# Router products in two halves of the array, row sums added up on VectorE, weight splits moved from GpSimd to VectorE, and one pool of eight PSUM banks

## The chip, the cores and the metric

The kernel runs on one core of one Trainium2 chip. The metric is the device time of one execution in microseconds (us). Below, PE is TensorE (its weight loads PEld), ACT is ScalarE, DVE is VectorE, POOL is GpSimd, and SP is the engine that issues most DMAs. The granted clock is the share of TensorE's full 2.4 GHz.

## The reference, cut to what matters

Two transformer blocks run in a row on 512 tokens of width 1024, in float32. The first block modulates and normalizes, mixes a dilated attention with a convolution, and ends in a mixture of 32 experts: a router picks one of 4 groups and two experts in it for each token, from a normalized row.

```
h2 = rms_norm(x, g_norm2) * (1 + sc2) + sh2
g_logits = h2 @ w_rg + b_rg          # 4 columns
e_logits = h2 @ w_re + b_re          # 32 columns
x = x + gt2 * hier_moe(h2, ...)
```

The second block puts 16 meta tokens in front (528 rows), runs a stick-breaking attention and a gated linear attention on projections of the same normalized rows, gates and mixes them, and adds the mix with a norm of its own; a convolutional feed-forward ends it.

```
mix = (gate_sb * (sb @ w_sb_out) + gate_gla * (o @ w_gla_out)) @ w_o
h = h + rmsnorm(mix, norm_mix_post)
```

Each rms norm needs the sum of squares over 1024 columns for every token.

## The kernel before, in words

Activations lie transposed: 8 tiles (m or k = 0 to 7) of 128 columns of the model by the tokens. Most products are made of three: a weight is split into a rounded high half on ACT (line 223) and the rest, its low half, on another engine (line 224, `ws.lo`), and so are the activations; high by high, high by low and low by high are added in PSUM (`mm3`, lines 310 to 312; line 1598 and 1620 for the projections). A plain float32 product goes to PE as two passes. Weights arrive through `Stream`: rings of 1 MB buffers that SP's DMAs fill as soon as a buffer comes free.

The order of instructions on each engine is settled when the program is built: a scheduler takes what is ready first by its estimates, in the order of the program where several are; a few places pin the order (`keep_in_program_order`) or raise a priority.

Four places matter.

The router (`router`, line 803) closes the first block's mixing. For each m, `ev_x1` makes xs (x scaled) and sq (x squared); `router` multiplies xs by 36 columns of router weights (line 808) and sq by ones, 32 columns wide, at partitions 64 to 95 of another bank (line 809), and both add up over m. `token_major` transposes xs on PE. At the end both sums are copied to `lgT`, and the selection of experts, a chain on DVE, begins; then come the experts, whose weights are some 196 MB from memory. Line 1206 multiplies there by two halves of 64 columns, line 1276 makes row sums with products of 32 columns.

After the experts the second block starts. Four splits of its value weights run through `ws` with the low half on POOL (line 1458 sets it; line 1731 sets it back to DVE); at the same time the scatter of the experts' rows (lines 1306, 1307, 1299), row sums (1276) and value products (`pva`, `pvb`) share PE, and `spread` (lines 1523 to 1529) distributes the row norms.

Then PSUM is laid out anew. Line 1733 opens a pool with four single banks (`p1`) and two pairs (`p2`). The first query and key projections (`pq`, line 1598, two banks each) are made in it by `need(("s", 0))`. Lines 2003 and 2004 close it and open one of eight single banks, and `weave` (line 2005) interleaves the stick-breaking chain (`sb_gen`: pz products, ACT and DVE work, psb products), the other projections (`qkg`, three steps to each step of the chain) and the gated attention.

Last, the mixing stage (`mix_mm`, `mix_out`, lines 2170 to 2199): for 8 m and two halves a of the tokens, 24 products give `pmix`; ACT copies it and squares it, and `su.flush` sums the squares of all m over the partitions through products of 128x128 ones (line 1643). The norm that comes of it (`su.rstd`) feeds the feed-forward.

Of the kernel before, what the change touches and what calls it, by code (L numbers as in the profile page):

```python
# [11 lines left out]
F32 = mybir.dt.float32  # L12
# [3 lines left out]
OP = mybir.AluOpType  # L16
# [4 lines left out]
P = 128  # L21
T = 512
D = 1024
KD = D // P
NM = 16
L = T + NM
# [5 lines left out]


COLS = [
    ("b_mod", 48), ("g_norm1", 8), ("conv_b", 4), ("conv_ln_g", 4), ("conv_ln_b", 4),
    ("conv_w", 4 * 31), ("g_norm2", 8), ("w_router", 8 * 36), ("c", 8),
    ("g_final", 8), ("norm_mix_pre", 8), ("b_gk", 4), ("gla_head_norm", 2),
    ("norm_mix_post", 8), ("norm_ffn_pre", 8), ("conv_w2", 22 * 3), ("conv_b2", 22),
]
# [132 lines left out]
def weave(*gens):  # L172

    live = [[t, dt, g] for g, t, dt in gens]
    while live:
        x = min(live, key=lambda q: q[0])
        x[0] += x[1]
        if next(x[2], x) is x:
            live.remove(x)
# [14 lines left out]
def build(nc, tc, I, out, dbg=None):  # L194
    with ExitStack() as ctx:
        _build(ctx, nc, tc, I, out, dbg or {})


def _build(ctx, nc, tc, I, out, dbg):
    mm = nc.tensor.matmul  # L200
    transpose = nc.tensor.transpose
    act = nc.scalar.activation
    tt = nc.vector.tensor_tensor
# [105 lines left out]
    def mm3(ps, lh, ll, rh, rl, first, last):  # L309
        mm(ps, lh, rh, start=first, stop=False)  # L310
        mm(ps, lh, rl, start=False, stop=False)  # L311
        mm(ps, ll, rh, start=False, stop=last)  # L312
# [10 lines left out]
    def cc(name, i=0, n=1):  # L323
        o = COFF[name][0] + i
        return cpk1[:, o:o + n] if o < NCOL1 else cpk2[:, o - NCOL1:o - NCOL1 + n]
# [5 lines left out]
    ones = const.tile([P, P], F32, name="ones")  # L331
# [44 lines left out]
    def p1(name="p1"):  # L376
        return pp.tile([P, 512], F32, name=name, tag="p1", bufs=4)
# [105 lines left out]
    ws = Stream(plan, castp, 3, nmoe)  # L483
# [62 lines left out]
    for k in range(KD):  # L546
        sq = big.tile([P, T], F32, name="sq", tag=("sq", "t512")[k % 2], bufs=2)
# [211 lines left out]
    wr = lambda k: cc("w_router", 36 * k, 36)  # L759
# [24 lines left out]
    plg = []  # L784
# [18 lines left out]
    def router(st):  # L803
        m, sq, xs = st
        if m == 0:
            plg.extend((p1("plg"), p1("plq")))
            act(rs_[:, 0, 0:1], sq[:, 0:1], AF.Sqrt)
        mm(plg[0][0:36, :], wr(m), xs, start=(m == 0), stop=(m == KD - 1), skip_group_check=True)
        mm(plg[1][64:96, :], ones[:, 0:32], sq, start=(m == 0), stop=(m == KD - 1), skip_group_check=True)
        if m < KD - 1:  # L810
            token_major(m, xs)

    def token_major(m, xs):
        pt = p1("pth")
        for i in range(4):
            s = slice(i * P, (i + 1) * P)
            transpose(pt[:, s], xs[:, s], ident)
        for a in range(2):
            (copy if m % 2 and m < KD - 1 else lambda o, x: act(o, x, AF.Copy))(
                h2t[a][:, :2 * D].rearrange("p (i d) -> p i d", d=D)[:, :, m * P:(m + 1) * P],  # L820
                pt[:, a * 256:(a + 1) * 256].rearrange("p (i n) -> p i n", n=P))
# [77 lines left out]
    for m in range(KD):  # L899
# [12 lines left out]
        behind = ev_x1(m, ps)  # L912
    next(mod)
    router(behind)
    for m in range(KD):
        dump(f"x1_{m}", xT[m])
# [4 lines left out]
    plg = p1("plgt")[:, :256].rearrange("p (i n) -> p i n", n=64)  # L921
# [320 lines left out]
    def weighted(psd, w, spare=False):  # L1242
        yh, yl = [(ep.tile([P, D], F32R, name="yx", tag="x", bufs=3) if spare else
                   yp.tile([P, D], F32R, name=n, tag=n)) for n in ("yh", "yl")]
        for n in range(2):
            s = slice(n * 512, (n + 1) * 512)
            act(yh[:, s], psd[n], AF.Copy, scale=w)  # L1247
            stt(yl[:, s], psd[n], w, yh[:, s].bitcast(F32), OP.mult, OP.subtract)  # L1248
        return yh, yl
# [64 lines left out]
    side, xs = [], {}  # L1314
# [99 lines left out]
    last = weighted(psd, wsl[:, q:q + 1])  # L1414
# [4 lines left out]
    with tc.For_i(0, n_over, 1) as o:  # L1419
# [5 lines left out]
        ws = Stream([(I["w_moe"][bass.ds(e, 1), i, :, :].rearrange("a p n -> (a p) n"), (2048,), False)  # L1425
                     for i in range(6)])
# [13 lines left out]
    ws = main  # L1440
# [14 lines left out]
                self.t = raw1.tile([P, 2048], dt, name="wsplit", tag="raw", bufs=2)  # L1455
            return self.t[:, :1024] if tag == "whi" else self.t[:, 1024:]

    ws.pool, ws.rc, ws.rings, ws.lo = Halves(), 2, ws.rings[:1], nc.gpsimd.tensor_tensor
    ws.rings[0][3], ws.pin = len(plan), nmoe + 1
    ws.hold_at(nmoe + 2)  # L1460
    ws.load()
# [103 lines left out]
    HP = ctx.enter_context(tc.tile_pool(name="H", bufs=1))  # L1565
# [7 lines left out]
    def t5(name, p=P):  # L1573
        return HP.tile([p, L], F32, name=name, tag="t5", bufs=4)
# [8 lines left out]
    def psum_pool(name, n1, n2):  # L1583
        st = ExitStack()
        pool = st.enter_context(tc.tile_pool(name=name, bufs=1, space=PSUM))
        q1 = lambda name="p1": pool.tile([P, 512], F32, name=name, tag="p1", bufs=n1)
        q2 = lambda name="p2": pool.tile([P, 2, 512], F32, name=name, tag="p2", bufs=n2)
        return st, q1, q2
# [38 lines left out]
    def part(ap, a):  # L1627
        return ap[:, E[a][0]:E[a][1]]

    class Sums:  # L1630
# [7 lines left out]
        def add(self, a, sq):  # L1638
            self.pend[a].append(sq)

        def flush(self, a):
            for sq in self.pend[a]:
                mm(self.ps[a], ones, part(sq, a), start=(self.n[a] == 0), stop=(self.n[a] == KD - 1))  # L1643
                self.n[a] += 1
            self.pend[a] = []

# [55 lines left out]
    def vproj():  # L1702

        pst = []

        def gen():
            pst.extend(p1("pv") for _ in range(5))
            yield from vproj_gen(nh, nl, xt, pst[:4], pst[4])

        return gen(), lambda dst: vproj_end(dst, pst[:4], pst[4], t5("tail")[:, :T], p1)  # L1710
# [8 lines left out]
    for k0 in (0, 4):  # L1719
        for x in (nh, nl):  # L1720
            for a in range(2):
                for k in range(4):
                    mm(pl[a][32 * k:32 * k + 32], w[:, k0 + k, :], x[k0 + k][:, a * HF:(a + 1) * HF].bitcast(F32),
                       start=(k0 == 0 and x is nh), stop=(k0 > 0 and x is nl), skip_group_check=True)
# [5 lines left out]
        act(glr[:, a * HF:(a + 1) * HF], pl[a], AF.Copy)  # L1730
    ws.lo = tt
    PB.close()
    PS, p1, p2 = psum_pool("psumC", 4, 2)
    wgk = cp.tile([P, 512], F32, name="wgk")
    nc.gpsimd.memset(wgk, 0.0)
    for g in range(0, P, 32):
# [192 lines left out]
    def sb_gen():  # L1929
        units = [(hp, j, b) for hp in range(4) for j in (4, 3, 2, 1, 0) for b in range(2)]  # L1930
        yield from pipeline(units, [sb_z, sb_soft, sb_cum, sb_sum, sb_exp, sb_out])
# [64 lines left out]
    def gla_gen():  # L1996
        units = [(g, li) for g in range(2) for li in range(7)]
        yield from pipeline(units, [gla_diff, gla_exp, gla_mul, lambda un, gf: att_mm(un[1], un[0], gf, gf)])
# [1 line left out]
    need(("s", 0))  # L2000
    gv0, gv0_end = vproj()
    gv1, gv1_end = vproj()
    PS.close()
    PS, p1, p2 = psum_pool("psumC2", 8, 0)
    weave((sb_gen(), 0, 1), (qkg, 0, 0.33), (gla_gen(), 6.6, 1.6), (sb_meta(), 32.5, 1.6),
          (gv0, 41, 0.1))
    dump("sbT", sbT)
# [7 lines left out]
    last = gv0_end(gv[:, 0])  # L2015
# [3 lines left out]
    last = gv1_end(gv[:, 1])  # L2019
# [71 lines left out]
    PS, p1, p2 = psum_pool("psumE", 0, 4)  # L2091
# [18 lines left out]
    for d in range(2):  # L2110
        sqs = []
# [5 lines left out]
        for a in range(2):  # L2117
            for h in range(4):
                mm(pn[32 * h:32 * h + 32, a, :H5], ones[:, 0:32], ends(sqs[h])[:, a], start=(d == 0), stop=(d == 1),
                   skip_group_check=True)  # L2120
# [43 lines left out]
    PS, p1, p2 = psum_pool("psumF", 4, 2)  # L2164
    t = p2("psum")
    su = Sums([t[:, 0], t[:, 1]])
    r = HP.tile([P, L], F32, name="rstd2", tag="rstd2", bufs=2)
    wo, pso, sqo = {}, {}, {}

    def mix_mm(m, a):  # L2170
        if m not in wo:
            wo[m] = ws.nxt(P)
            sqo[m] = t5("sq")
        wh, wl = wo[m]
        ps = pso[m, a] = p1("pmix")[:, :E[a][1] - E[a][0]]
        for kk in range(KD):
            mm3(ps, wh[:, kk, :], wl[:, kk, :], part(mh[kk], a), part(ml[kk], a), kk == 0, kk == KD - 1)

    def mix_out(m, a):
        ps = pso.pop((m, a))  # L2180
        act(part(mx[m], a), ps, AF.Copy, scale=cc("norm_mix_post", m))
        act(part(sqo[m], a), ps, AF.Square)
        su.add(a, sqo[m])

    for m in range(KD - 2):
        for a in range(2):
            mix_mm(m, a)
            su.flush(a)
        for a in range(2):
            mix_out(m, a)  # L2190

    for a in range(2):
        for m in (KD - 2, KD - 1):
            mix_mm(m, a)
            su.flush(a)
            mix_out(m, a)
        su.flush(a)
        with tc.high_priority(offset=100):
            su.rstd(a, r, D)
# [8 lines left out]
    def h_gen(a):  # L2208
        for k in range(KD):
            with tc.high_priority(offset=200):  # L2210
                t, h, g = cp.tile([P, T], F32, name="t", tag="y", bufs=3)[:, :E[a][1] - E[a][0]], part(hT[k], a), cc("norm_ffn_pre", k)
                tt(t, part(mx[k], a), part(r, a), OP.mult)
                (nc.gpsimd.tensor_tensor if k in HPL else tt)(h, h, t, OP.add)
                act(part(nh[k], a), h, AF.Copy, scale=g)
                stt(part(nl[k], a), h, g, part(nh[k], a).bitcast(F32), OP.mult, OP.subtract)
            sq = t5("sq")
            act(part(sq, a), h, AF.Square)
            su.flush(a)
            su.add(a, sq)
            if k == KD - 1:  # L2220
                su.flush(a)
            yield
# [130 lines left out]
    su = Sums([p1("psum"), p1("psum")])  # L2353
# [29 lines left out]
```

## Time and profile before

| | |
|---|---|
| three runs | 1812.36, 1812.47, 1816.58 us; median 1812.47 |
| the profiled execution | 1818.69 us, span 1816.9 |
| PE busy | 1745.1 us, 96% of the span |
| DVE, ACT, POOL busy | 881.3, 629.3, 109.6 us |
| mean granted clock of PE | 0.978 |
| memory traffic | 322 MB read, 180 GB/s over the span |

The span is the time from the first to the last instruction of the profiled execution. A busy PE counts matmuls that overlap in its pipeline, so a matmul's duration is longer than its step: products of 512 columns that stand one behind the other have durations of about 0.4 us and starts 0.23 us apart. In a row of a timeline, the bracket at the end gives the idle time of the engine before the instruction and what ended it; several equal instructions are merged (x2). In a table of stretches the columns are the busy time of each engine with its number of instructions, the granted clock, the share of the DMA engines and GB/s. In a list of waits the numbers are the total, the count and the longest.

### The profile page before, as it was taken

To read this page: it belongs to the slowest core of one execution; us is meant where nothing else is said; L and a number is where in the kernel's file an instruction comes from. 1 tells how busy PE (TensorE), PEld (TensorE's weight loads), DVE (VectorE), ACT (ScalarE), POOL (GpSimd) and SP (SyncE) were. 2 spreads that over 40 slices of the span, in tenths; PEclk is the share of its full clock that TensorE was granted. 3 is DMA by queue.
4 is the path that set the end of the run, shared out by engine and by line. 5 is a ranking of instruction groups with operands and counts; after the bars stand their busy time and mean duration, and the time that the engine had idled before them with its cause. 6 is when DMAs were issued, how large, how long until landed. Compare 5 with 4: busy or idle time off the path is not lost.

```text
span 1816.9 us, 26870 instructions
## 1 busy us (share of the span) xinstructions
PE 1745.1 (96%) x10826; PEld 1263.2 (70%) x10826; DVE 881.3 (49%) x1597; ACT 629.3 (35%) x1141; POOL 109.6 (6%) x147
## 2 busy tenths in 40 slices
PE   7999997999999999998899999999999999999997
PEld 4776565444445444445788668989999899789985
DVE  6789654433333334235577742253332645335534
ACT  5226653211111111104567743242233633223322
POOL 2000010000000000003200100030000111001101
PEclk9989898999999999999999999999999999999998
DMA  8563253999999999930411012113222222222221
GB/s 327 199 242 136 89 216 130 380 409 409 408 411 360 385 408 410 412 128 27 159 67 49 24 47 93 47 63 128 102 100 87 70 91 78 100 93 93 94 87 64
DMA packets 73986, 328.01 MB, mean 181 GB/s; under 512 B 8019, under 2 KB 8403, under 8 KB 59652
## 3 DMA queue, kind: packets, MB, share of 16 engines
q1 hardware_dynamic: 72608, 320.36, 46.6%
q0 software_dynamic: 1248, 5.91, 0.9%
q8 instruction: 86, 1.41, 0.3%
q14 instruction: 40, 0.33, 0.0%
q10 hardware_dynamic: 4, 0.00, 0.0%
HBM read 321.98 MB, written 4.26 MB: 180 GB/s over the span
## 4 chain that ended last, share of the span: by engine, by line
PE 48%; DVE 3%; ACT 2%; DMA 1%; POOL 1%; issue 1%; DVEq 0%; ACTq 0%; POOLq 0%
PE p L1620 11%; PE pup L2232 7%; PE pq L1598 4%; PE pg L312 2%; PE pg L310 2%; PE pg L311 2%; PE pd L311 2%; PE pd L312 2%; PE pd L310 2%; PE pv L310 1%; PE pv L311 1%; PE pv L312 1%; PE pmix L310 1%; PE psum L1643 1%; PE pmix L312 1%; PE pmix L311 1%
## 5 line engine op out<-in xcount | busy, mean ns | idle before, releaser
L224 DVE TENSOR_TENSOR wsplit<-raw,wsplit 128x1024 fp32r<-128x1024 f32 (+1 forms) x140 | 167.4, 1198 | 250.6 <-ACT wsplit L223 244.7
L223 ACT ACTIVATE wsplit<-raw 128x1024 fp32r<-128x1024 f32 (+1 forms) x144 | 146.8, 1022 | 260.5 <-PE pd L312 76.3
L1206 PE MATMUL pgu<-raw,x 128*64 128x512 f32 x960 | 220.3, 598 | 0.0
L1206 PEld LDWEIGHTS pgu<-raw,x 128*64 128x64 f32 x960 | 64.1, 136 | 119.9 <-issue 106.4
L1299 DVE SCALAR_TENSOR_TENSOR x<-psx,modc,x 128x512 f32<-128x512 f32 x136 | 93.2, 745 | 50.1 <-PE psx L1307 50.0
L1248 DVE SCALAR_TENSOR_TENSOR yl<-pdn,wsl,yh 128x512 fp32r<-128x512 f32 x34 | 25.4, 751 | 178.8 <-ACT yh L1247 178.3
L1206 PE MATMUL pdn<-raw,hT 128*64 128x512 f32 x480 | 105.7, 593 | 0.7 <-ACT hT L1228 0.7
L1228 ACT ACTIVATE hT<-pht 128x512 f32<-128x512 f32 x17 | 10.2, 597 | 232.0 <-PE pht L1222 227.5
L1206 PEld LDWEIGHTS pdn<-raw,hT 128*64 128x64 f32 x480 | 34.5, 137 | 69.1 <-issue 64.4
L647 DVE SCALAR_TENSOR_TENSOR y<-u,cpk,y 128x512 f32<-128x512 f32 x116 | 80.6, 748 | 0.1
L311 PE MATMUL pd<-wsplit,ah 128*128 128x512 f32 x176 | 71.1, 404 | 2.1 <-DVE wsplit L224 2.0
L1168 PE MATMUL psg<-oh,h2h 128*128 128x256 f32 (+1 forms) x288 | 67.8, 292 | 3.1 <-DVE oh L1153 3.1
L1620 PE MATMUL p<-nha,wsplit 128*128 128x258 f32 x384 | 69.0, 293 | 1.3 <-ACT wsplit L223 0.7
L312 PE MATMUL pd<-wsplit,al 128*128 128x512 f32 x176 | 70.1, 398 | 0.0
L310 PE MATMUL pd<-wsplit,ah 128*128 128x512 f32 x176 | 68.9, 397 | 0.9 <-ACT wsplit L223 0.9
L1168 PE MATMUL psg<-oh,h2l 128*128 128x256 f32 (+1 forms) x288 | 65.7, 282 | 0.0
L1620 PE MATMUL p<-nhb,wsplit 128*128 128x258 f32 x384 | 65.6, 283 | 0.0
L2232 PE MATMUL pup<-nha,wsplit 128*128 128x258 f32 x352 | 64.0, 291 | 0.4 <-ACT wsplit L223 0.4
L1306 PE MATMUL psx<-ohT,yh 128*128 128x512 f32 x136 | 59.3, 436 | 5.2 <-ACT wsplit L223 5.1
L2232 PE MATMUL pup<-nhb,wsplit 128*128 128x258 f32 x352 | 63.2, 287 | 0.0
L1168 PEld LDWEIGHTS psg<-oh,h2h 128*128 128x128 f32 x288 | 53.6, 196 | 9.7 <-issue 5.7
L1620 PEld LDWEIGHTS p<-nha,wsplit 128*128 128x128 f32 x384 | 56.2, 195 | 3.0 <-ACT wsplit L223 0.9
(653 smaller groups left out, 3973.5 us busy)
## 6 DMA issues: line engine op xcount, KB each, us to landing
raw<-w_moe SPq DMA_DIRECT2D x312, 512.0 KB, 10.1
raw<-w_moe SPq DMA_DIRECT2D x36, 1024.0 KB, 10.0
raw<-w_ff SPq DMA_DIRECT2D x22, 1024.0 KB, 4.8
raw<-w_mod SPq DMA_DIRECT2D x16, 1024.0 KB, 5.9
raw<-w_qk SPq DMA_DIRECT2D x12, 1024.0 KB, 5.1
raw<-w_v SPq DMA_DIRECT2D x8, 1024.0 KB, 4.9
raw<-w_modk SPq DMA_DIRECT2D x8, 1024.0 KB, 5.2
raw<-w_mg SPq DMA_DIRECT2D x8, 1024.0 KB, 4.9
```

Source lines behind the costliest of these rows:

```text
L223: act(hi, src, AF.Copy)
L224: return sub(lo, src, hi.bitcast(F32), OP.subtract)
L310: mm(ps, lh, rh, start=first, stop=False)
L311: mm(ps, lh, rl, start=False, stop=False)
L312: mm(ps, ll, rh, start=False, stop=last)
L647: tap[0] = stt(y[:, m, :], src, w, y[:, m, :], OP.mult, OP.add)
L1168: fix(mm(ps[k // 2][:, k % 2 * 256:][:, :n], w[i][:, k * P:(k + 1) * P], oh[:, i, :n], start=(i == 0 and w is h2h and k % 2 == 0), stop=(i ...
L1206: fix(mm(ps[s, :], l[:, s], w[:, 2 * b + i, :], start=first, stop=last, skip_group_check=True))
L1299: stt(xT[m], ps, gt2(m), xT[m], OP.mult, OP.add)
L1598: mm(ps[a], l[:, kk, :], r[kk][:, a * HF:(a + 1) * HF], start=(kk == 0 and fl == 0), stop=(kk == k - 1 and fl == 2))
L1620: mm(ps[a], l[:, kk, :], ends(r[kk])[:, a], start=(kk == 0 and fl == 0), stop=(kk == k - 1 and fl == 2))
L2232: mm(ps[:, a, :HC], l[:, kk, :], x[kk][:, o:o + HC], start=(kk == 0 and fl == 0), stop=(kk == KD - 1 and fl == 2))
```

## The change

The constants' columns are put in another order, so that 64 columns can be read from any router block. The router's two products become 64 columns wide each. The low halves of the four weight splits go to DVE. The pool of line 1733 has eight single banks, and the second pool is not opened. In the mixing stage DVE adds the squares of m = 1 to 5 to the tile of m = 0, which lies in another buffer; that tile, m = 6 and m = 7 go through the products with ones; the flag that closes a sum is given by the caller instead of counted.

```diff
-        mm(plg[0][0:36, :], wr(m), xs, start=(m == 0), stop=(m == KD - 1), skip_group_check=True)
-        mm(plg[1][64:96, :], ones[:, 0:32], sq, start=(m == 0), stop=(m == KD - 1), skip_group_check=True)
+        mm(plg[0][0:64, :], cc("w_router", 36 * m, 64), xs, start=(m == 0), stop=(m == KD - 1), skip_group_check=True)
+        mm(plg[1][64:128, :], ones[:, 0:64], sq, start=(m == 0), stop=(m == KD - 1), skip_group_check=True)
...
-    ws.pool, ws.rc, ws.rings, ws.lo = Halves(), 2, ws.rings[:1], nc.gpsimd.tensor_tensor
+    ws.pool, ws.rc, ws.rings, ws.lo = Halves(), 2, ws.rings[:1], tt
...
-        def flush(self, a):
+        def flush(self, a, last=True):
             for sq in self.pend[a]:
-                mm(self.ps[a], ones, part(sq, a), start=(self.n[a] == 0), stop=(self.n[a] == KD - 1))
+                mm(self.ps[a], ones, part(sq, a), start=(self.n[a] == 0), stop=last)
...
-    PS, p1, p2 = psum_pool("psumC", 4, 2)
+    PS, p1, p2 = psum_pool("psumC", 8, 0)
...
-    PS.close()
-    PS, p1, p2 = psum_pool("psumC2", 8, 0)
...
-            sqo[m] = t5("sq")
+            sqo[m] = t5("sq") if m else HP.tile([P, L], F32, name="sqs", tag="rstd2", bufs=2)
...
-        su.add(a, sqo[m])
+        if 0 < m < KD - 2:
+            tt(part(sqo[0], a), part(sqo[0], a), part(sqo[m], a), OP.add)
+        if m == 0 or m == KD - 2:
+            su.pend[a] = [sqo[0]] if m == 0 else su.pend[a] + [sqo[m]]
+        elif m == KD - 1:
+            su.add(a, sqo[m])
...
         for a in range(2):
             mix_mm(m, a)
-            su.flush(a)
...
         for m in (KD - 2, KD - 1):
             mix_mm(m, a)
-            su.flush(a)
+            su.flush(a, False)
             mix_out(m, a)
```

## Rows read from the trace of the kernel before

**Rows 1.** The page: busy time, share of the span and instructions of each engine.
```profile
PE 1745.1 (96%) x10826; PEld 1263.2 (70%) x10826; DVE 881.3 (49%) x1597; ACT 629.3 (35%) x1141; POOL 109.6 (6%) x147
```
**Rows 2.** PE's waits over the whole span: us in total, times, longest us.
```profile
PE psx L1306 <- ACT wsplit L223: 5.1, 1, 5.1
...
PE psum L1643 <- ACT sq L2182: 2.1, 1, 2.1
...
PE pz L1856 <- ACT ahi L223: 0.8, 1, 0.8
```
**Rows 3.** Timeline of PE, router for one m: start, us, instruction.
```profile
262.37 1.05 PE L808 MATMUL plg<-xs,cpk 128*36 128x512 f32 x2
263.35 1.04 PE L809 MATMUL plq<-sq,ones 128*32 128x512 f32 x2
264.33 0.66 PE L817 MATMUL pth<-ident,xs 128*128 128x128 f32 x4
```
**Rows 4.** Timeline of PE, four row sums of 32 columns at line 1276.
```profile
831.91 0.62 PE L1276 MATMUL pss<-sq,ones 128*32 128x512 f32 x1
...
831.93 0.62 PE L1276 MATMUL pss<-sq,g2r 128*32 128x512 f32 x1
832.36 0.59 PE L1276 MATMUL pss<-sq,ones 128*32 128x512 f32 x1
...
832.91 0.50 PE L310 MATMUL pva<-wsplit,uh 128*128 128x512 f32 x1
```
**Rows 5.** The page's costliest groups: count, busy us, mean ns, idle us.
```profile
L1206 PE MATMUL pgu<-raw,x 128*64 128x512 f32 x960 | 220.3, 598 | 0.0
```
**Rows 6.** Timeline of all engines at the router's last two products.
```profile
289.36 1.05 PE L808 MATMUL plg<-xs,cpk 128*36 128x512 f32 x2
...
290.31 0.72 ACT L796 ACTIVATE xs<-x,a 128x512 f32<-128x512 f32 x1 [6.90 <-DVE x L793]
...
292.88 1.05 PE L808 MATMUL plg<-xs,cpk 128*36 128x512 f32 x2
```
**Rows 7.** Busy time by stretch, router to expert stage.
```profile
260.00:280.00 20.00, 20.00 (x79) 11.70 (x78) 5.89 (x9) 7.15 (x12) 0.00 (x0) 1.00 0.28 101
280.00:300.00 20.00, 15.47 (x62) 8.08 (x60) 7.07 (x23) 7.29 (x13) 3.62 (x10) 0.98 0.13 42
...
340.00:380.00 40.00, 40.00 (x206) 18.50 (x206) 11.21 (x21) 6.11 (x13) 0.00 (x0) 1.00 1.02 397
```
**Rows 8.** Timeline, the loads of expert weights issued behind the router.
```profile
296.29 29.68 SPq L272 DMA_DIRECT2D raw<-w_moe  x10
```
**Rows 9.** The chain of waits in the mixing stage: one of its twelve pieces of 0.43 or 0.44.
```profile
1387.09 0.44 PE psum L1643 x2
```
**Rows 10.** Timeline of DVE in and behind the mixing stage.
```profile
1379.00 1.23 DVE L224 TENSOR_TENSOR wsplit<-raw,wsplit 128x1024 fp32r<-128x1024 f32 x1 [5.31 <-ACT wsplit L223]
...
1411.83 0.42 DVE L2213 TENSOR_TENSOR hTb<-hTb,t 128x260 f32<-128x260 f32 x1
```
**Rows 11.** Timeline of all engines at the fourth weight split.
```profile
846.99 2.38 POOL L224 TENSOR_TENSOR wsplit<-raw,wsplit 128x1024 fp32r<-128x1024 f32 x1 [6.05 <-ACT wsplit L223]
...
847.35 2.05 DVE L1292 TENSOR_TENSOR rs__80<-rs__80 128x4 f32<-128x4 f32 x1
...
850.27 1.10 PE L1529 MATMUL pspread<-dg,ones 128*128 128x512 f32 x2 [1.22 <-DVE dg L1526]
```
**Rows 12.** The chain of waits ahead of the stick-breaking chain's first product.
```profile
882.87 2.27 DMA c_tge<-tge
```
**Rows 13.** Timeline of PE: the first projection, and the first stick-breaking product.
```profile
871.75 0.48 PE L1598 MATMUL pq<-nha,wsplit 128*128 128x264 f32 x2 [1.09 <-DVE x L1666]
...
886.08 0.22 PE L1810 MATMUL pz<-sqk 64*16 64x16 f32 x4 [2.30 <-ACT sqk L1772]
```
**Rows 14.** Busy time by stretch, behind that product and near the weave's end.
```profile
886.00:890.00 4.00, 3.92 (x22) 3.88 (x23) 2.82 (x6) 1.93 (x8) 3.93 (x9) 0.57 0.27 80
...
1040.00:1050.00 10.00, 9.22 (x29) 4.38 (x28) 5.69 (x17) 7.17 (x19) 0.00 (x0) 0.67 0.00 0
```

More of the change, by code (lines that the diff above doesn't have):

```diff
@@ L34 @@
 COLS = [
-    ("b_mod", 48), ("g_norm1", 8), ("conv_b", 4), ("conv_ln_g", 4), ("conv_ln_b", 4),
-    ("conv_w", 4 * 31), ("g_norm2", 8), ("w_router", 8 * 36), ("c", 8),
+    ("b_mod", 48), ("g_norm1", 8), ("w_router", 8 * 36), ("conv_b", 4), ("conv_ln_g", 4), ("conv_ln_b", 4),
+    ("conv_w", 4 * 31), ("g_norm2", 8), ("c", 8),
     ("g_final", 8), ("norm_mix_pre", 8), ("b_gk", 4), ("gla_head_norm", 2),
@@ L2217, in h_gen @@
             act(part(sq, a), h, AF.Square)
-            su.flush(a)
+            su.flush(a, False)
             su.add(a, sq)
```

## The prediction

> **What bounds the kernel now.** I read the page first, then the waits of TensorE, then the stages that the diff touches as timelines and as tables of busy time, and the chain of waits last. The reader is to see that PE is busy 96% of the span [rows 1], and that once the expert stage runs PE's own waits are few and short: the longest are 5.1 us and then 2.3 and less, and in most of the long second block under 1 [rows 2, 13]. So an instruction that leaves PE's queue is worth its time where PE does not wait, and a wait that leaves is worth its length and what the clock loses behind it.
>
> The profiled execution took 1818.69 us, its span 1816.9; the three runs have their median at 1812.47. The sum is made in microseconds of that execution and taken off the median; in none of the stages below do I see where the 6 us between the two lie.
>
> **Router (lines 808, 809).** Eight times, for each m, PE runs two float32 products of two passes each. The 36-column one starts at 262.37, the 32-column one at 263.35, the transposes behind them at 264.33: 0.98 us each, one after the other [rows 3]. The change makes both 64 columns wide, for partitions 0 to 63 and 64 to 127. What such neighbours cost is seen in the row sums at line 1276: of four products of 32 columns all first passes start between 831.91 and 831.93, the second ones 0.45 later, and the next ordinary product starts at 832.91, so four together cost the 1.0 us of one [rows 4]. The expert products at line 1206 are 64 wide and in pairs, as the new ones are: 960 passes, 598 ns each in the mean, are busy 220.3 us together, 0.23 us a pass, half of 0.45 [rows 5]. So a pair should cost 0.98 instead of 1.96. For m = 0 to 5 that is 6 x 0.98 = 5.9 us. At the last pair its inputs come into it: xs ends at 290.31 + 0.72 = 291.03. Before, the stretch from 289.36 (the product for m = 6) to the end of the last (292.88 + 0.98) is 4.50; after it, a pair takes 0.98 and the transposes 0.6, then the last pair cannot start before about 291.3 and ends at 292.3. That saves 1.6 [rows 6]. Of the sum of 7.5 I take 7.4, a tenth less for loading 64 columns instead of 36. The bounds are 0.8 (no overlap, only the pause between two widths goes, 0.1 a product at most as 0.98 is more than two passes of 0.45) and 7.8.
>
> From 260 to 280 PE is busy 20 of 20 us, DVE and ACT 6 and 7, so nothing else is late next [rows 7]. Does the gain survive the expert stage, where DMA is saturated (share 1.02)? From 260 to 300 the DMA share is 0.28 and 0.13, the rings are full [rows 7]. The next ten loads start at 296.29, when the router's end has freed their space, and behind the first five each waits for PE to use up weights [rows 8]. All of it starts earlier by the same 7.4, so the saturated stage moves as a block.
>
> **Row sums in the mixing stage (lines 2170 to 2199).** Before, the square of each of 8 m and 2 halves goes through a float32 product with ones: 16 calls. After, DVE adds the squares of m = 1 to 5 to that of m = 0, and 3 calls remain for each half. A call costs 0.44 us in the chain of waits [rows 9]. 10 x 0.44 = 4.4 us, all of it ahead of the stage's end, where PE has its one long wait, 2.1 us for ACT's last square [rows 2]; that square hangs on PE's last product and moves with it. DVE gets 10 additions of 0.42 us; in each m it sits idle some 5 us until ACT's split [rows 10]. If that cover were gone, two additions would hold the next weight split back by 0.8. Bounds 3.6 (one call of each half falls into an idle place) to 4.9.
>
> **Low halves of four weight splits (line 1458), from POOL to DVE.** POOL takes 2.38 us for one [rows 11], DVE 1.23 [rows 10]. The first three lie beside PE's work: two come where DVE waits for the first scatter product, the third where PE has products in hand. The fourth, 846.99 to 849.37, matters. During it a DVE operation on 128x4 takes 2.05 us and ends with it, at 849.40; the diagonal for the spread comes late, and PE waits 1.22 us [rows 11]. After, DVE does the split itself: ahead of that operation it ends at 846.99 + 1.23 = 848.2 and the operation near 848.5, and PE's wait shrinks by 0.9; behind it, the wait is gone, 1.2. The gain travels on, as DVE's normalization waits for the second spread product on PE. Queued behind the four splits on DVE are the x updates and the low halves of the activations; if PE waits once for an update behind a whole split, that costs 1.2. I take 1.0; bounds -1.2 to 2.0.
>
> **Eight banks from the first projection on (line 1733).** This pool had four single banks, and four in pairs that nobody takes. The first query and key projections fill the four. PE has finished them at 883.8 and waits 2.30 us, until 886.08, for ACT's copy of the key [rows 13]; ACT has stood behind a constant whose table lands at 882.87 + 2.27 = 885.14 [rows 12]. The next projection, which could run meanwhile, writes to banks of the old pool and starts only behind the wait. With eight banks it finds two that nobody reads. PE's order is fixed when the program is built, by estimated readiness; I expect projection steps in front of the first stick-breaking product as far as the builder sees the gap, a copy of about 1 us. After the wait the granted clock is 0.57 for 4 us, mostly the lower level of 1.2 GHz: 1.7 us lost, which a shorter gap may keep [rows 14]. The gap and its clock are 2.3 + 1.7 = 4.0; the first projection waits 1.09 for the last x update on DVE, by way of a bank I think, and that may go too [rows 13]: at most 5.1. From below, the new order may hand the stick-breaking chain its products later: -2. I take 1.7, a step of 1 us and some of the clock.
>
> The rearranged constants add no instruction; the columns read past the last router block end in rows that no one copies.
>
> **Sum.** 7.4 + 4.4 + 1.0 + 1.7 = 14.5 us: 1804.2 for an execution like the profiled one, 1798.0 against the median.
>
> **Rivals.**
> (a) The second product's first pass starts only when the first one's second pass has begun. A pair then costs three passes, 0.98 + 0.45 = 1.43, and saves 0.53: 8 x 0.53 = 4.2, in all 11.3, 1801.2. For it: the two write to different banks, the sums at line 1276 to one. Against: there, no second pass starts ahead of any first one [rows 4]. The Trainium skill says in "TensorE: Matmul & The Clock Gate", section "Step-by-step: what each phase is for", that matmuls stay in program order and only weight loads are pulled ahead; read strictly, with each product's two passes adjacent, it makes this rival, and rows 4 disagree with it.
> (b) The pair does not overlap at all and the router edit gives 0.8: in all 7.9, 1804.6. Only the different banks speak for it.
> (c) The bank edit does not do what it says: the projection stays behind the wait. In all 12.8, 1799.7, inside the forecast's own range.
> (d) New orders on PE, ACT and DVE between 860 and 1080, which follow from the new pool, give back 9 to 14 us: 1807 to 1812, no change. Behind 890 PE's longest wait there is 0.8 [rows 2], so a new order has little to lose or win.
> (e) Slower: in the same stage the projections run ahead of the stick-breaking chain as far as eight banks allow, four of them at 6.0 us (871.75 to 883.8 hold two [rows 13]). The chain goes to and fro between ACT, DVE and PE; it then ends the stage with PE out of other work, 24 us idle and 1.7 for the clock, against 12.8 saved elsewhere: +13, 1825. It decides from the point where more than two projections stand in front of the first stick-breaking product. For it: at 1040 to 1050, near the chain's end, PE already runs at 0.67 of its clock [rows 14]. Against: the weave takes three projection steps to each step of the chain, whatever the banks.
>
> **How the numbers follow.** The forecast with (c) holds 0.72, at 1792 to 1804: its terms' better bounds (7.8, 4.9, 2.0, 5.1) make 19.8, and the worse ones of all but the router (3.6, -1.2, -2.0) with 7.4 make 7.8, which I cut to 8.5 as they won't all meet. (a) 0.09, (b) 0.06, (d) 0.09, (e) 0.04. The predicted time is 1798.0. The range of 1791 to 1806 takes in the forecast, (a) and (b), and leaves out (d), (e) and a little of the edges. A measurement of this kernel tells about 0.3%, 5.4 us, from no change, so faster is below 1807.0: the forecast, (a) and (b), 0.87. The same: (d), 0.09. Slower: (e), 0.04.
>
> **What would show it.** Passes of lines 808 and 809 that start in pairs, 0.98 us from the pair to the transposes, and the ten loads near 288.9 instead of 296.29; 44 passes on line 1643 instead of 64; no line 224 on POOL, and the 128x4 operation behind the fourth split at a tenth of its 2.05; projection steps between the key's last product and the first stick-breaking product, and a clock above 0.57 behind it. The prediction is wrong if the router's products still stand 0.98 apart, if the expert stage takes longer from its start than before, or if the stretch from the first projection to the weave's end grows.

## The result, and the profile after

The changed kernel ran in 1802.31 us (median of 8 runs, 1793.64 to 1815.05), where the kernel before ran in 1812.7 beside it: a ratio of 0.9938 over all the runs (95% interval 0.9911 to 0.9965; the two medians alone give 0.9943), 11.2 us less (6.3 to 16.1). The prediction said 1798.0, in a range of 1791 to 1806. Two later comparisons of the same two kernels gave 0.9909 (0.9878 to 0.9941) and 0.9921 (0.9893 to 0.9948).

The profiled execution of the changed kernel took 1800.42 us, its span 1798.6. Against the one of before (1818.69, 1816.9) that is 18.3 us, more than the runs differ by, so the profiles can't be compared by their totals; they are compared stretch by stretch below. The page's first part, PE and POOL (busy us, share, instructions), answers to [rows 1]:

```profile
PE 1726.9 (96%) x10806; PEld 1255.9 (70%) x10806; DVE 883.2 (49%) x1611; ACT 629.0 (35%) x1141; POOL 102.8 (6%) x143
```

PE has 20 passes less and POOL four instructions less, DVE 14 more. The timeline of PE in the router for one m (start, us, instruction; compare [rows 3]):

```profile
259.16 0.64 PE L809 MATMUL plg<-xs,cpk 128*64 128x512 f32 x1
259.17 0.64 PE L810 MATMUL plq<-sq,ones 128*64 128x512 f32 x1
259.64 0.59 PE L809 MATMUL plg<-xs,cpk 128*64 128x512 f32 x1
259.64 0.59 PE L810 MATMUL plq<-sq,ones 128*64 128x512 f32 x1
260.17 0.66 PE L818 MATMUL pth<-ident,xs 128*128 128x128 f32 x4
```

Both first passes start within 0.01 us of each other, then both second ones, and the transposes follow 1.01 behind the pair, where two products took 1.96. SP's timeline shows the ten loads behind the router, 296.29 in [rows 8]:

```profile
283.27 30.39 SPq L272 DMA_DIRECT2D raw<-w_moe  x10
```

The row sums (line 1644) have 40 and 4 passes; the rows give their durations in ns (min, median, max) and the first and last start:

```profile
L1644 PE MATMUL psum<-sq,ones x40: 377/381/488, 1384.6 to 1412.0; 128*128 128x260 f32 x20, 128*128 128x256 f32 x20
...
L1644 PE MATMUL psum<-sqs,ones x4: 378/380/386, 1381.3 to 1388.7; 128*128 128x260 f32 x2, 128*128 128x256 f32 x2
```

DVE's timeline at the fourth weight split (compare [rows 11]): the split stands ahead of the operation on 128x4 (line 1293 here, 1292 before), which takes 0.17 us instead of 2.05.

```profile
834.39 1.23 DVE L224 TENSOR_TENSOR wsplit<-raw,wsplit 128x1024 fp32r<-128x1024 f32 x1 [1.65 <-ACT wsplit L223]
835.53 0.17 DVE L1292 RECIPROCAL rs__80<-rs__80 128x4 f32<-128x4 f32 x1
835.74 0.17 DVE L1293 TENSOR_TENSOR rs__80<-rs__80 128x4 f32<-128x4 f32 x1
```

PE's timeline at the first stick-breaking product (compare [rows 13]): the wait for the key's copy is 0.64 instead of 2.30, but no step of the next projection stands in front of it.

```profile
870.90 0.40 PE L1599 MATMUL pq<-nhb,wsplit 128*128 128x264 f32 x2
871.94 0.22 PE L1811 MATMUL pz<-sqk 64*16 64x16 f32 x4 [0.64 <-ACT sqk L1773]
```

**The same stretches in every profile.** Starts of the same two instructions of PE, subtracted, in us. Router: from the first product of line 808 to the first transpose behind the routing logits (plgt). Spread: from the first spread product to the first low-rank product (pl). Projection: from its first pass to the first stick-breaking product (pz). Chain: from that product to the first psb product. Mixing: from the first output product (pmix) to the first of the next stage (pup).

| profile | router | spread | projection | chain | mixing |
|---|---|---|---|---|---|
| before | 42.46 | 12.33 | 14.33 | 19.37 | 52.45 |
| router edit alone (e1) | 35.19 | 12.33 | 13.64 | 17.88 | 52.47 |
| row sums alone (e2) | 42.46 | 12.33 | 13.73 | 19.42 | 48.25 |
| low halves alone (e3) | 42.46 | 11.10 | 13.93 | 17.88 | 52.47 |
| eight banks alone (e4) | 42.46 | 12.32 | 14.14 | 19.39 | 52.47 |
| whole change | 35.19 | 11.10 | 14.12 | 17.88 | 48.25 |
| whole change (e5) | 35.19 | 11.10 | 14.05 | 17.88 | 48.24 |
| whole change (e9) | 35.19 | 11.10 | 14.14 | 17.87 | 48.25 |

Three of the columns (router, spread, mixing) repeat to 0.02 us, and each moves with one edit: 42.46 - 35.19 = 7.27, 12.33 - 11.10 = 1.23, 52.47 - 48.25 = 4.22, together 12.7 us. The projection's column lies between 13.6 and 14.3 with the eight banks and without them. The chain's column has two values, 17.9 and 19.4: the higher one is that of executions whose granted clock falls behind the first stick-breaking product, as it does in [rows 14]. All four profiles here with the low halves on DVE have the lower one, and of the four without only e1; e3 below takes this up.

**Where the rest of the 18.3 lies.** The first 250 us have the same program in both kernels, and yet the router's first product starts at 252.15 before and at 246.43 after. The busy time of the stretch from 180 to 230 us, in the attention stage (us of the stretch; busy PE, weight loads, DVE, ACT, POOL; granted clock, DMA share, GB/s), for the kernel before, the changed one, and the changed one in the profile e9:

```profile
180.00:230.00 50.00, 45.53 (x244) 28.77 (x244) 31.37 (x81) 30.22 (x76) 0.00 (x0) 0.83 0.27 105
```
```profile
180.00:230.00 50.00, 44.47 (x247) 27.89 (x247) 35.60 (x89) 31.41 (x79) 0.00 (x0) 0.97 0.39 152
```
```profile
180.00:230.00 50.00, 44.71 (x229) 30.22 (x229) 27.91 (x76) 27.73 (x73) 0.00 (x0) 0.73 0.22 84
```

The granted clock was 0.83, 0.97 and 0.73 there: time at 1.2 instead of 2.4 GHz that one execution of this program gets and another doesn't. In e9 the router starts at 257.69, 11.3 us later than in the first profile of the same kernel. That is as large as what the change is worth, so only many runs, or one stretch, can weigh it. Of the 18.3 us between the profiles, 5.7 lie ahead of the router, 12.7 in the three columns and 1.5 in the chain's; that is 19.9, and the stretches between them give 1.6 back.

### The profile page after: what moved, and what is told of

It is laid out like the page before. It is cut to its first block, busy times and chain, and to the rows that moved or that the text cites. A ratio compares the mean times of both kernels' runs of the same rounds, so it can differ in the third digit from the quotient of the medians.

```text
span 1798.6 us, 26848 instructions
## 1 busy us (share of the span) xinstructions
PE 1726.9 (96%) x10806; PEld 1255.9 (70%) x10806; DVE 883.2 (49%) x1611; ACT 629.0 (35%) x1141; POOL 102.8 (6%) x143
## 4 chain that ended last, share of the span: by engine, by line
PE 49%; DVE 3%; ACT 2%; POOL 1%; issue 0%; DVEq 0%; ACTq 0%; POOLq 0%
PE p L1621 11%; PE pup L2235 7%; PE pq L1599 5%; PE pg L312 2%; PE pg L310 2%; PE pg L311 2%; PE pd L311 2%; PE pd L312 2%; PE pd L310 2%; PE pv L310 1%; PE pv L312 1%; PE pv L311 1%; PE pmix L310 1%; PE pmix L312 1%; PE pmix L311 1%; PE psb L1892 1%
## 5 line engine op out<-in xcount | busy, mean ns | idle before, releaser
L224 DVE TENSOR_TENSOR wsplit<-raw,wsplit 128x1024 fp32r<-128x1024 f32 (+1 forms) x144 | 171.6, 1195 | 230.2 <-ACT wsplit L223 223.9
```

The source lines that it names most:

```text
L224: return sub(lo, src, hi.bitcast(F32), OP.subtract)
```

## The experiments

**e1, the router edit alone.**

```diff
-        mm(plg[0][0:36, :], wr(m), xs, start=(m == 0), stop=(m == KD - 1), skip_group_check=True)
-        mm(plg[1][64:96, :], ones[:, 0:32], sq, start=(m == 0), stop=(m == KD - 1), skip_group_check=True)
+        mm(plg[0][0:64, :], cc("w_router", 36 * m, 64), xs, start=(m == 0), stop=(m == KD - 1), skip_group_check=True)
+        mm(plg[1][64:128, :], ones[:, 0:64], sq, start=(m == 0), stop=(m == KD - 1), skip_group_check=True)
```

> The router edit alone on the kernel before. Theory A (each edit takes its own time out of TensorE's queue, and nothing else of the program matters): 7.5 us less from the router's start to its end (pairs 4.40 us apart for each m instead of 5.35), carried unchanged through the expert stage, so 1805.2 against 1812.7, a ratio of 0.9959. Theory C (the early start is given back where DMA is saturated, which is why the whole change measures 11 and not 14): the router ends 7.5 us early but the expert stage grows by 3, so 1808. If the profile shows a gain of 7.5 at the first ten loads and the same 7.5 at the end of the expert stage, C is out.

Measured: 1805.66, ratio 0.995 (0.993 to 0.997). The ten loads start at 283.43. From 320 to 820 us every product of PE starts 12.1 us earlier than in the profile before, the same to 0.1: the expert stage moves as a block, and theory C is out. At the router's end it was 12.8 (5.6 from before the router, 7.3 from it); the 0.7 goes ahead of 320, as it does in e4 (from 4.5 to 3.8 against the profile before), which lacks the router edit.

**e2, the row sums alone.**

```diff
+        if 0 < m < KD - 2:
+            tt(part(sqo[0], a), part(sqo[0], a), part(sqo[m], a), OP.add)
...
             mix_mm(m, a)
-            su.flush(a)
```

> Only the row sums of the mixing stage. Theory A: 10 products fewer on line 1643 (54 against 64 in the three sums together), 4.2 us less in the mixing stage and nothing elsewhere: 1808.5, ratio 0.9977. Theory C: the additions on VectorE hold weight splits back, and the stage gains under 3: 1810 or more. The 2.1 us wait for the last square stays in both.

Measured: 1808.63, ratio 0.9976 (0.9956 to 0.9995). The number in the expectation was wrong: this kernel has the 44 passes of the whole change, not 54, as ten calls of two passes go. 4.22 us go, as theory A has it. In DVE's timeline the additions lie in idle places and the weight split behind them waits only for ACT:

```profile
1372.44 0.42 DVE L2184 TENSOR_TENSOR sqs<-sqs,sq 128x256 f32<-128x256 f32 x1 [2.40 <-ACT sq L2182]
1373.39 1.23 DVE L224 TENSOR_TENSOR wsplit<-raw,wsplit 128x1024 fp32r<-128x1024 f32 x1 [0.52 <-ACT wsplit L223]
```

**e3, the low halves alone.**

```diff
-    ws.pool, ws.rc, ws.rings, ws.lo = Halves(), 2, ws.rings[:1], nc.gpsimd.tensor_tensor
+    ws.pool, ws.rc, ws.rings, ws.lo = Halves(), 2, ws.rings[:1], tt
```

> Only the low halves of four weight splits from POOL to VectorE. Theory A: TensorE's wait of 1.2 us before the first spread product goes, 1.2 to 1.6 us less between 845 and 860, 1811.3, not to be told from no change by the times, only by the stage in the profile. Theory D (the low halves also set when the hTd store lands, and so whether the key's copy is late): the wait before the first stick-breaking product falls from 2.30 to under 1 as in the whole change, and the gain is 3 or more.

Measured: 1814.69, ratio 1.0006 (0.9986 to 1.0026): no change that the times show; 1.23 us in the spread stretch. The wait before the first stick-breaking product is 0.64 here, without any bank edit, as theory D has it for the wait. But the times show no gain of 3; their interval leaves room for 2.5 at most. PE's timeline:

```profile
870.53 0.78 PE L1598 MATMUL pq<-nha,wsplit 128*128 128x264 f32 x2 [1.08 <-DVE x L1666]
...
884.46 0.22 PE L1810 MATMUL pz<-sqk 64*16 64x16 f32 x4 [0.64 <-ACT sqk L1772]
```

and the busy time of the stretch that the projection begins in:

```profile
870.00:874.00 4.00, 3.47 (x17) 3.50 (x18) 2.65 (x3) 1.44 (x2) 0.55 (x1) 0.57 1.00 385
```

The projection's first passes run at a granted clock of 0.57, mostly 1.2 GHz ("the half clock" from here on), so it ends later, and the wait behind it is shorter by about as much. What this buys comes behind the wait. The busy time of the four microseconds there, in e3 and in e4, the next experiment, which keeps the low halves on POOL:

```profile
885.00:889.00 4.00, 4.00 (x35) 4.00 (x35) 1.38 (x3) 1.18 (x7) 2.27 (x5) 1.00 0.59 158
```
```profile
883.00:887.00 4.00, 4.00 (x22) 4.00 (x21) 2.24 (x6) 1.16 (x7) 3.36 (x7) 0.57 0.44 109
```

e4 has the half clock there, like the kernel before [rows 14], and e3 has full clock. So the half clock has moved to a place where the wait for the table hides most of its cost, and the first psb product comes 17.88 us behind the first stick-breaking product, not 19.37 as before: 1.5 us, on top of the 1.23. The rows of that psb product, before and in e3:

```profile
905.45 0.29 PE L1891 MATMUL psb<-z,sv 16*64 16x16 f32 x4
```
```profile
902.34 0.29 PE L1891 MATMUL psb<-z,sv 16*64 16x16 f32 x4
```

All eight profiles with this edit have full clock behind that product, and one of the six without it, e1. Why the half clock moves with the edit stays open.

**e4, the eight banks alone.**

```diff
-    PS, p1, p2 = psum_pool("psumC", 4, 2)
+    PS, p1, p2 = psum_pool("psumC", 8, 0)
...
-    PS.close()
-    PS, p1, p2 = psum_pool("psumC2", 8, 0)
```

> Only the eight banks. On all five engines the program is the same instructions in the same order with the same waits as before; only bank numbers differ. Theory A: no change, 1812.7 within 0.3%, and the wait before the first stick-breaking product stays near 2.3 us where the hTd store lands as late as before. Theory B (the bank edit itself shortened that wait to 0.64 in the whole change and kept the clock behind it): the wait is near 0.6 and the stretch from the first projection to the weave is 1.7 to 3.2 us shorter, 1810.

Measured: 1814.1, ratio 1.0006 (0.999 to 1.0023). Theory A. The timelines of PE, POOL and ACT:

```profile
882.30 0.22 PE L1810 MATMUL pz<-sqk 64*16 64x16 f32 x4 [2.04 <-ACT sqk L1772]
```
```profile
878.73 0.56 POOL L1680 DMA_DIRECT2D c_ntri<-ntri  x1 [9.87 <-DMA hTd<-x]
879.28 0.55 POOL L1680 DMA_DIRECT2D c_tge<-tge  x1
```
```profile
881.38 0.31 ACT L1689 ACTIVATE mtger<-c_tge 128x128 fp32r<-128x128 f32 x1 [0.47 <-DMA c_tge<-tge]
881.60 0.65 ACT L1772 ACTIVATE sqk<-pq 128x264 f32<-128x264 f32 x2
```

The wait's length is told by POOL: it issues the table's load only when the hTd store has landed, after 9.87 us of idleness, and the key's copy stands behind the table on ACT. Without the half clock in front, the projection's products end before that and PE waits (1.6 to 2.4 us in five profiles without the low-halves edit besides that of before); with it they end about when the table is there.

**e5 and e9, the whole change again.**

> The whole change again, with a second profile. Theory A (additive): the product of the four single ratios, 0.995 x 0.9976 x 1.0006 x 1.0006 = 0.9938, 1801.5 against 1812.7. If the edits gave something back to each other, it would be 0.996 or more. The wait before the first stick-breaking product, 0.64 in the first profile, is not fixed by the program: I expect 0.6 to 2.3, set by when the hTd store lands.

> The whole change a third time, on the same chip as the three kernels beside it, so that the next two can be set against it: 1800 to 1803, the wait before the first stick-breaking product 0.6 to 2.3.

Measured: 1799.91 and 1800.1, ratios 0.9909 (0.9878 to 0.9941) and 0.9921 (0.9893 to 0.9948). The product of the four single ratios, 0.9938, and the 12.7 us of the stretches, 0.9930, lie in all three intervals; so does 0.9922, the 12.7 us and the chain's 1.5 together. The wait was 0.6 all three times, not spread over 0.6 to 2.3 as expected.

**e8 and e12, one product of the router widened, the other left.**

```diff
 e8
+        mm(plg[0][0:64, :], cc("w_router", 36 * m, 64), xs, start=(m == 0), stop=(m == KD - 1), skip_group_check=True)
         mm(plg[1][64:96, :], ones[:, 0:32], sq, start=(m == 0), stop=(m == KD - 1), skip_group_check=True)
 e12
         mm(plg[0][0:36, :], wr(m), xs, start=(m == 0), stop=(m == KD - 1), skip_group_check=True)
+        mm(plg[1][64:128, :], ones[:, 0:64], sq, start=(m == 0), stop=(m == KD - 1), skip_group_check=True)
```

> The kernel before with the router's first product 64 columns wide and the second left at 32 (partitions 64 to 95). Theory W (two products lie beside each other only if both are of one width): 0.98 from the first to the second, no pairs, 5.35 us for each m, gain under 0.8. Theory P (disjoint column groups are enough): they start together, 4.40 us for each m, gain 7.5. The trace of before, 36 beside 32, speaks for neither.

> The kernel before with the router's first product left at 36 columns and the second 64 columns wide (partitions 64 to 127). 64 beside 32 gave no pairs (0.98 each). Theory W (both must be of one width): none here, 5.35 us for each m. Theory V (36 columns take a group of 64, and that is what counts): pairs, 4.40 for each m and 7.5 less at the router's end.

PE's timeline of e8, and that of e12:

```profile
262.37 1.07 PE L808 MATMUL plg<-xs,cpk 128*64 128x512 f32 x2
263.38 1.04 PE L809 MATMUL plq<-sq,ones 128*32 128x512 f32 x2
264.35 0.66 PE L817 MATMUL pth<-ident,xs 128*128 128x128 f32 x4
```
```profile
260.85 0.62 PE L808 MATMUL plg<-xs,cpk 128*36 128x512 f32 x1
260.86 0.64 PE L809 MATMUL plq<-sq,ones 128*64 128x512 f32 x1
261.31 0.59 PE L808 MATMUL plg<-xs,cpk 128*36 128x512 f32 x1
261.34 0.59 PE L809 MATMUL plq<-sq,ones 128*64 128x512 f32 x1
261.86 0.66 PE L817 MATMUL pth<-ident,xs 128*128 128x128 f32 x4
```

64 beside 32 stays one after the other (router stretch 42.67), 36 beside 64 pairs (35.19, the whole gain), in one profiled execution each. Theory V: 36 columns count as a group of 64, and what kept the two apart was the 32 of the second. The Trainium skill says in "TensorEngine Tiling (Array Packing)", section "Key Properties", that a change of the tiling mode, unlike one of the tile alone, drains the engine. Both timelines agree as far as they go: the products of e8 stand one behind the other and those of e12 do not, while a drain as such shows in neither. The wider first product, and with it the rearranged constants, were not needed.

**e6, two more edits to the changed kernel.**

```diff
+    tge = HP.tile([P, P], F32, name="c_tge")
+    nc.gpsimd.dma_start(tge, I["tge"])
...
     hTd = dr.tile([P, 2, 4, L], F32, name="hTd")
...
+            if 0 < k < KD - 2:
+                nc.gpsimd.tensor_tensor(part(sqh, a), part(sqh, a), part(sq, a), OP.add)
```

> The kernel after with two more edits. First, the table c_tge, its negative and the constant of -1 get a place of their own, so that their load and copies no longer wait for the hTd store. Theory E (the wait before the first stick-breaking product is ACT standing behind that store): the wait is the copy alone, 0.6 to 0.7, in whatever execution. Theory B (it is about banks): it stays spread from 0.6 to 2.3. Second, the squares of the next stage (line 2220) are added up too, on POOL, so that line 1644 has 24 passes and not 44: TensorE-bound there, 10 x 0.44 = 4.4 us less between 1395 and 1415; if POOL's additions (0.9 each) hold the residual additions of the same engine back, TensorE waits for the normalized rows and under 2 us are left. Together 0.4 to 2 and 4.4: 1796 to 1797 against 1802 for the kernel after.

Measured: 1808.15, ratio to the kernel before 0.9957 (0.9938 to 0.9977): worse than the change. The second edit is a loss. PE's waits (us, times, longest), and the timeline of POOL:

```profile
PE psum L1644 <- POOL sqh L2225: 3.5, 2, 2.6
```
```profile
1400.23 6.55 POOL L2225 TENSOR_TENSOR sqh<-sqh,sq 128x260 f32<-128x260 f32 x5 [1.57 <-ACT sq L2223]
1406.74 0.91 POOL L2219 TENSOR_TENSOR hTa<-hTa,t 128x256 f32<-128x256 f32 x1
```

All ten additions of POOL (shortest, median, longest in ns):

```profile
L2225 POOL TENSOR_TENSOR sqh<-sqh,sq x10: 787/814/3009, 1400.2 to 1415.2; 128x260 f32<-128x260 f32 x5, 128x256 f32<-128x256 f32 x5
```

The row of five took 6.55 us, where five at 0.9 make 4.5: its first addition took 3.01, the other four 0.80 to 0.82. Why the first took so long stays open. The residual addition stands behind them, and PE waits for the sums. Between 1390 and 1420 the kernel falls 6.8 us behind the changed one; a part of that is a stretch from 1402 to 1405 at half clock, which the changed kernel's first profile does not have there. The first edit settles nothing: the wait was 0.6, as expected, but it was so in the changed kernel's three profiles too.

**e7 and e10, two projection steps in front.**

```diff
+    for _ in range(2): next(qkg)
     weave((sb_gen(), 0, 1), (qkg, 0, 0.33), (gla_gen(), 6.6, 1.6), (sb_meta(), 32.5, 1.6),
```

> The kernel after, with two steps of the next projection asked for ahead of the weave, so that twelve of its products stand in front of the first stick-breaking product on TensorE: what the prediction took the eight banks to do. Theory F (the step in the prediction was right but for the order): the wait before the first stick-breaking product falls by up to 1.5 us, to 0 to 0.8, the clock behind it stays at 1.00, and the stretch up to the weave's end shrinks by 1 to 2. Theory G (the chain behind it only starts later): the wait goes but comes back further on, no change in the stretch.

> The kernel with two projection steps (twelve products) in front of the first stick-breaking product, again, with five rounds. Theory F: 1 us better than the kernel after, as the first look at its trace has it between 870 and 900, so 1800 to 1801 where the kernel after has 1801.5; what its first median showed beyond that (1793.8 of five) was the granted clock. Theory H (work in that place also keeps the clock up later in the stage): 3 or more, and again no drop of the clock between 1030 and 1050.

Twelve more products now stand ahead of the first stick-breaking product. PE's timeline in e7:

```profile
877.19 0.40 PE L1599 MATMUL pq<-nha,wsplit 128*128 128x264 f32 x2
877.53 0.22 PE L1811 MATMUL pz<-sqk 64*16 64x16 f32 x4
```

The wait is gone (0.9 in e10, where the projection ran at full clock and the table came late). From 850 to 900 us PE gains 0.7 and 0.9 on the changed kernel's first profile, theory F. Measured: 1793.78, ratio to before 0.9876 (0.9847 to 0.9905), and 1795.97, 0.9902 (0.987 to 0.9934). Against all 21 runs of the changed kernel the 11 runs have a ratio of 0.9975 (0.9958 to 0.9992, by drawing the runs anew 20,000 times, chips thrown together): 4.5 us, of which the traces show under one. Both profiles lack the drop of the clock between 1030 and 1050 that two of the changed kernel's have, but its third, e9, lacks it too, so theory H isn't shown. It is the fastest version here; where the rest comes from stays open.

**e11, the same two steps with the old pools of banks.**

> The router, low halves and row sums of the change with the old pools of banks, and the same two projection steps asked for ahead of the weave. The old pool must be empty before the new one opens, so all 48 products of that projection, and not twelve, stand in front of the first stick-breaking product. Theory F: the wait is gone here too, but the chain of exponentials starts 4.4 us later (36 more products at 0.122); if that chain has slack, as TensorE's short waits behind 890 say, the stage ends as with eight banks, 1800 to 1802. Theory I (rival e of the prediction in small: the chain ends the stage): the stage ends up to 4 us later, 1805.

Measured: 1802.25, ratio to before 0.9924 (0.9895 to 0.9953), the changed kernel's own time. All 48 products stand in front; the first stick-breaking product starts 20.0 us behind the projection's first pass, not 14.1, and still behind a wait of 0.64, for a copy of the second projection (gq), which theory F had gone:

```profile
863.43 0.78 PE L1598 MATMUL pq<-nha,wsplit 128*128 128x264 f32 x2 [1.09 <-DVE x L1666]
...
883.44 0.22 PE L1810 MATMUL pz<-sqk 64*16 64x16 f32 x4 [0.64 <-ACT gq L1772]
```

At 900 us PE is 0.3 behind the changed kernel, and no more by 1030: the chain has slack, and theory I is out.

## Why the prediction was right or wrong

- **Router, 7.4: right.** 7.27. Pairs start together and take 1.01 to the transposes, and the stretch for one m falls from 5.35 to 4.40. Rivals (a) and (b) fell, as both second passes start at 259.64. Passes in strict program order, as the prediction read the Trainium skill for rival (a), are not what these rows show. But the prediction gave no reason why 36 and 32 don't overlap; e8 and e12 do. The expert stage moved as a block, as it said.
- **Row sums, 4.4: right.** 4.22, ten calls, all additions in DVE's idle places, and the wait of 2.1 for the last square is still there.
- **Low halves, 1.0: right in place and size, but not the whole of it.** 1.23 in the spread stretch, with the split ahead of the small operation. What the prediction didn't see lies behind it. Seven of the eight profiles with this edit (all but e10) have the half clock at the start of the first projection, none of the six without; five of those six (all but e1) have it behind the first stick-breaking product instead, none of the eight with the edit. At the projection's start it costs 1.3 us and takes about as much off the next wait; behind the product it costs 1.5 (19.4 against 17.9). So in the profiles this edit is worth 2.7 us, a little more than the 2.5 for which the times of e3 leave room.
- **Eight banks, 1.7: wrong.** The step that failed is "I expect projection steps in front of the first stick-breaking product as far as the builder sees the gap". With the bank edit alone the traces have the same instructions in the same order on all five engines, and the time is the same, a ratio of 1.0006: rival (c). The banks were not what kept the projection behind: the weave asks for the stick-breaking product first. Asked for earlier (e7, e10), steps go in front; and only then do the banks matter, as they let twelve products pass and not 48 (e11). The shorter wait and the full clock behind it in the profile after, which look like the predicted gain and are signs that the prediction named, belong to the low halves (e3). Rivals (d) and (e) fell with the step that they rest on.
- **The sum, 14.5: close by luck.** The three columns give 12.7, as the banks' 1.7 fell away and the other terms' errors cancel to 0.1. The chain's 1.5 brings it to 14.2, in the place and nearly the size of the banks' term, but from another edit. The runs' 11.2 (6.3 to 16.1) doesn't tell the two sums apart. The 6 us between the profiled execution of before and its median, which the prediction didn't find, have a likely place between 190 and 210, where that execution lost 4 to 5 us to the clock; other executions lost it there as well, so this is argued, not shown.

## What to carry to other kernels

Here two products on column groups of one size ran side by side, and only the narrower one had to be widened, so look for neighbours of unequal width before changing the layout. More banks changed nothing until the order of the program used them: compare the order of instructions of both kernels first, and count an edit that leaves it alone at zero. A wait that shrinks in one profile isn't the edit's doing until the edit alone shows it. And the edit that took one wait away here also moved a drop of the clock some way behind it, so read the clock behind the place that was changed as well.

## What the runs showed of the hardware that was not expected

- 36 columns pair with 64, and 64 don't with 32: 1.01 for a pair against 1.98 (e12, e8).
- Taking PE's wait of 1.2 us ahead of the spread products away was followed, some 20 us later, by 3 to 4 us at 1.2 GHz behind waits of 1.3 and 1.1 that were there before too, at full clock; the 3 to 4 us at 1.2 GHz behind the first stick-breaking product, which e4 has, were not there (e3 against e4).
- One stretch of 50 us of one program had a granted clock of 0.97 and 0.73 in two executions, and the code up to the router took 11.3 us longer in the second.
- POOL's first addition on 128x260 in a row of five took 3.01 us, the next four 0.80 to 0.82 (e6); alone such an addition took 0.85 to 0.93 (e6, and the changed kernel).
